# Attention values in three 64-column matmuls, with one operation that scales and evicts

## The chip, the cores and the metric

The kernel runs on one NeuronCore of a Trainium2 chip. The metric is device time in microseconds (us), the median of several executions; smaller is better. Engines are named as in the profile: PE is TensorE (matmuls), PEld its weight loads, DVE is VectorE, ACT is ScalarE, POOL is GpSimd, SP is the queue engine that issues nearly all DMA transfers.

## The reference

One encoder layer on x of 2048 x 1024 float32. What matters here is the attention with a forget gate, 16 heads of 64:

```python
def block(args):                       # one block of 128 queries
    logits = (jnp.einsum('bqhd,bkhd->bhqk', q_i, k).astype(jnp.float32) * scale
              + (F_i[..., :, None] - F[..., None, :]))
    logits = jnp.where(k_pos[None, :] <= q_pos[:, None], logits, -jnp.inf)
    p = jax.nn.softmax(logits, axis=-1).astype(v.dtype)
    return jnp.einsum('bhqk,bkhd->bqhd', p, v)
...
x = x + g_m * fox_mixer(h, ...)
x = x + g_f * (jnp.square(jax.nn.relu(h @ w_mlp_in[i])) @ w_mlp_out[i])
```

## The kernel before, in words

Float32 products are made from operands that are split into a high and a low part, and three of the four partial products are added up in PSUM: high by high, high by low, low by high.

The program has two stretches. The first, to about 1509 us of the span, holds the attention. Heads go in eight pairs g. For each pair a sweep over the 2048 rows (`sweep`, L497 to L499) projects rows to q, k and v; the row operands are split by ACT (L416) and POOL (L417). Beside it runs `attention`: for each block i of 128 queries and each head h of the pair, `att_scores` multiplies q with k (L547, L548, a mask at L550) and DVE adds the forget terms and takes row maxima (L554), `att_exp` makes exponentials on ACT (L565, and the float16 high part `ph` at L572), `att_transpose` makes the low part on DVE (L584) and transposes both parts by DMA into `pT` (L592, issued by SP), and `att_values` multiplies them with the values. The second stretch is the dense MLP; the change touches no line of it.

In `att_values` the tile v holds 128 columns for a head: 64 of the values' high part, then 64 of their low part, all float16. For each block b of 128 keys PE loads the transposed high part of the probabilities and multiplies it with all 128 columns (L610), then loads the low part and multiplies it with the 64 high columns alone (L611). So the high by low product gathers in 64 columns of its own. When both heads of a pair are through, DVE adds the two column groups out of PSUM (`tensor_reduce`, L619), and a second operation multiplies with the reciprocal row sums (L621), on POOL for the pairs 0 to 6 and on DVE for the pair 7. A DMA on SP then writes `ot` to `o_d` (L623). The accumulator `po` has two slots, and `pT` has five buffers (NPT = 5): the sixth transpose must wait until PE has read the first.

The order of instructions on each engine is made by a scheduler in the framework, which models durations and moves instructions by priority and readiness; each engine then executes its list in order. Priorities are set by `pri(n)`, and the values' matmuls have offset 0 (PR_PO), the scores' 100 (PR_S). So an edit of one operation can move others, too.

Of the kernel before, what the change touches and what calls it, by code (L numbers as in the profile page):

```python
# [17 lines left out]
F32 = mybir.dt.float32  # L18
# [4 lines left out]
ALU = mybir.AluOpType  # L23
AX = mybir.AxisListType
# [3 lines left out]
P = 128  # L28
# [4 lines left out]
HD = 64  # L33
# [5 lines left out]
NG = NH // 2  # L39
# [21 lines left out]
def fox_layer(ctx, tc, x, c, norm_mix, norm_mlp, w_ada, b_ada, w_mlp_in, w_mlp_out,  # L61
              fox_w_in, fox_b_f, fox_q_norm, fox_k_norm, fox_w_out, out):
    nc = tc.nc
    x = x[0]
    out = out[0]
# [79 lines left out]
    def pri(n):  # L145
        return tc.high_priority(offset=n)
# [38 lines left out]
    with ExitStack() as st:  # L185
        psS = st.enter_context(tc.tile_pool(name="psS", bufs=2, space=PSUM))
        psT = st.enter_context(tc.tile_pool(name="psT", bufs=1, space=PSUM))
        psO = st.enter_context(tc.tile_pool(name="psO", bufs=1, space=PSUM))
# [405 lines left out]
            return pts  # L594

        po_of, n_po = {}, [0]
        po_all = psO.tile([P, 2, 2, P], F32, tag="O", name="po")

        def att_values(g, i, h, st, pts):
            nb = i + 1  # L600
            if h == 0:
                po_of[g, i] = po_all[:, n_po[0] % 2]
                n_po[0] += 1
            po = po_of[g, i]
            for b in range(nb):
                v = vT[g, b // RB][:, b % RB, h, :]
                pT, bb = pts[b * P // PW], b % (PW // P)
                nw = min(PW // P, nb - b + bb)
                with pri(PR_PO):
                    nc.tensor.matmul(po[:, h, :], lhsT=pT[:, bb, :], rhs=v, start=(b == 0), stop=False)  # L610
                    nc.tensor.matmul(po[:, h, 0:HD], lhsT=pT[:, nw + bb, :], rhs=v[:, 0:HD],  # L611
                                     start=False, stop=(b == nb - 1))
                if b % RB == RB - 1:
                    yield
            if h == 1:
                ot = sb.tile([P, 2, HD], F32, tag="ot", name=f"ot{g}_{i}", bufs=2)
                with pri(PR_OT):
                    nc.vector.reciprocal(st[:, 4:6], st[:, 2:4])
                    nc.vector.tensor_reduce(out=ot, in_=po.rearrange("p h (b d) -> p h d b", b=2), axis=AX.X,  # L619
                                            op=ALU.add)  # L620
                (nc.vector if g == NG - 1 else nc.gpsimd).tensor_tensor(  # L621
                    ot, ot, st[:, 4:6].unsqueeze(2).to_broadcast([P, 2, HD]), op=ALU.mult)
                nc.sync.dma_start(o_d[i][:, g * P:(g + 1) * P], ot.rearrange("p h d -> p (h d)"))  # L623
                del po_of[g, i]

        def attention():
            prev, late = None, []
            per = [C0 + 34.0 * (i + 1) for i in range(NT)]
            tot = 2.0 * sum(per)
            for g in range(NG):  # L630
                for i in range(NT):
                    st_ = sb.tile([P, 6], F32, tag="st", name=f"st{g}_{i}", bufs=6)
                    for h in range(2):
                        L = big(f"L{g}_{i}_{h}")
                        pv = iter(())
                        while len(late) > (LAG_S if i < 8 else LAG_L):
                            for _ in pv:
                                pass
                            pv = att_values(*late.pop(0))
                        nch = i // RB + 1  # L640
                        yield (g, i // RB), per[i] / tot / nch
                        for n, _ in enumerate(att_scores(g, i, h, st_, L)):
                            next(pv, None)
                            if n < nch - 1:
                                yield (g, i // RB), per[i] / tot / nch
                        if prev is not None:
                            late.append((*prev[:4], att_transpose(*prev[:3], *prev[4:])))
                        prev = (g, i, h, st_, L, att_exp(g, i, h, st_, L))
                        for _ in pv:
                            pass  # L650
            late.append((*prev[:4], att_transpose(*prev[:3], *prev[4:])))
            while late:
                for _ in att_values(*late.pop(0)):
                    pass
# [52 lines left out]
        for n, (need, dp) in enumerate(attention()):  # L707
# [3 lines left out]
            while need not in done or p_sw < p_att + (min(LEAD, LEAD0 + LEAD * p_att) if p_att < TAPER else LEAD1):  # L711
                d = next(stream, None)
# [421 lines left out]
    for p in range(NE):  # L1134
        a, b = ops.pop((0, "P1", p))
# [153 lines left out]
    for n, st_ in enumerate(steps):  # L1289
        s, prod, p = st_  # L1290
# [12 lines left out]
        if p == 0:  # L1303
            odd = (n // FP) % 2
            for tb in range(RB):
                pool, tag = (psS, "S") if not odd else ((psQ, "Q"), (psT, "T"))[tb // 2]
# [8 lines left out]
        for tb in range(RB):  # L1315
            for q in range(FP - END, FP) if final and p == FP - 1 else (p,):
                a, b = ops[s, prod, q]
# [34 lines left out]
```

## Time and profile before

| what | value |
|---|---|
| median of 3 runs | 2952.03 us (2948.38 to 2961.26) |
| the profiled execution's own time | 2949.7 us |
| its span, first to last instruction | 2948.0 us |
| busy share of the span: PE, PEld, DVE, ACT, POOL | 90%, 76%, 73%, 56%, 51% |
| granted TensorE clock over the span | 0.963 |

Busy shares are means over two stretches with different limits, so the attention is read by itself in what follows, from 124 us (first value matmul) to 1509 us (last eviction). Matmuls overlap in the array, so the duration of one is longer than the distance from its start to the start of the next; where a cost on PE is meant, the distance between starts is what counts.

### The profile page before, as it was taken

What the parts mean: (1) busy time and instruction counts of PE and PEld (TensorE: products, weight loads), DVE (VectorE), ACT (ScalarE), POOL (GpSimd) and SP (SyncE); (2) the same over time, 40 slices, a digit from 0 to 9 for tenths busy, and PEclk for the clock granted to TensorE, in tenths of its full rate; (3) what the DMA queues carried; (4) which work ended last, traced back from release to release, by engine and by line L of the source; (5) the groups of instructions that cost most, each with busy time, mean ns of one, the idle gap of its engine ahead of it and who ended that gap; (6) DMA issues with size and microseconds to landing.
All of it is one profiled execution on the core that took longest, in us unless ns stands there. A gap on an engine that the chain in (4) does not pass through costs nothing. (4 is left out here: it accounts for less than half of the span.)

```text
span 2948.0 us, 46378 instructions
## 1 busy us (share of the span) xinstructions
PE 2664.8 (90%) x15819; PEld 2231.8 (76%) x15819; DVE 2150.5 (73%) x3695; ACT 1646.8 (56%) x2899; POOL 1509.0 (51%) x1116
## 2 busy tenths in 40 slices
PE   4689888888988899888799999998999999999999
PEld 3677777777777787777678778876888878888887
DVE  6679887898878787887823486667556576875677
ACT  4466666667666676776624256644555444444433
POOL 2354454645445464644533565585654484730464
PEclk9799999998999999999899999999999999999999
DMA  8479999999999999897977867697665684555434
GB/s 283 127 169 191 211 210 210 204 206 209 214 202 216 200 207 200 182 202 161 210 207 234 264 225 236 208 337 238 202 196 175 224 276 126 157 164 169 128 120 155
DMA packets 921070, 593.73 MB, mean 201 GB/s; under 512 B 596276, under 2 KB 776572, under 8 KB 920832
## 3 DMA queue, kind: packets, MB, share of 16 engines
q1 hardware_dynamic: 917248, 578.44, 76.9%
q0 software_dynamic: 3584, 12.32, 1.2%
q8 instruction: 124, 2.03, 0.3%
q14 instruction: 114, 0.93, 0.1%
HBM read 338.81 MB, written 109.19 MB: 152 GB/s over the span
## 5 line engine op out<-in xcount | busy, mean ns | idle before, releaser
L584 DVE SCALAR_TENSOR_TENSOR ph<-L,ph 128x1024 f16<-128x1024 f32 (+7 forms) x384 | 435.0, 1144 | 80.8 <-ACT ph L572 78.9
L417 POOL TENSOR_TENSOR hl<-hl,hh 128x1024 fp32r<-128x1024 f32 x120 | 298.8, 2491 | 250.2 <-ACT hh L416 217.8
L572 ACT ACTIVATE ph<-L 128x1024 f16<-128x1024 f32 (+7 forms) x384 | 302.2, 804 | 172.8 <-DMA pT<-ph 142.8
L497 PE MATMUL psq<-w,hh 128*128 128x384 f32 (+1 forms) x960 | 343.1, 358 | 27.5 <-DVE v L506 12.3
L554 DVE CUSTOM_DVE_ANT_0 L<-S,F 128x1024 f32<-128x1024 f32 (+7 forms) x384 | 343.6, 905 | 22.4 <-PE S L548 8.3
L499 PE MATMUL psq<-w,hl 128*128 128x384 f32 (+1 forms) x960 | 354.6, 371 | 4.5 <-POOL hl L417 4.4
L565 ACT ACTIVATE L<-L,st 128x128 f32<-128x128 f32 (+15 forms) x256 | 306.9, 1199 | 84.9 <-DVE st L559 80.3
L498 PE MATMUL psq<-w,hh 128*128 128x384 f32 (+1 forms) x960 | 342.4, 359 | 6.6 <-POOL w L343 6.6
L142 PE MATMUL yP<-obP,oaP 128*128 128x512 f32 x880 | 343.3, 390 | 3.9 <-DVE obP L757 3.9
L143 PE MATMUL yP<-obP,oaP 128*128 128x512 f32 x880 | 342.5, 389 | 0.0
L141 PE MATMUL yP<-obP,oaP 128*128 128x512 f32 x880 | 338.1, 389 | 2.0 <-ACT obP L756 2.0
L610 PE MATMUL po<-v,pT 128*128 128x128 f16 x2176 | 274.7, 227 | 64.4 <-DMA pT<-ph 56.6
L757 DVE TENSOR_TENSOR oaP<-aP,oaP 128x512 fp32r<-128x512 f32 x220 | 219.6, 998 | 143.9 <-ACT oaP L756 143.7
L547 PE MATMUL S<-kT,qT 128*128 128x512 f32 (+3 forms) x640 | 260.2, 408 | 65.8 <-DVE mx L554 58.4
L756 ACT CAST oaP<-aP 128x512 fp32r<-128x512 f32 x220 | 137.1, 623 | 290.4 <-PE yP L143 275.1
L610 PEld LDWEIGHTS <-pT 128*128 128x128 f16 x2176 | 203.1, 102 | 95.0 <-DMA pT<-ph 67.0
L611 PE MATMUL po<-v,pT 128*128 128x64 f16 x2176 | 257.0, 200 | 0.0
L548 PE MATMUL S<-kT,qT 128*128 128x512 f32 (+3 forms) x640 | 239.6, 382 | 0.0
L611 PEld LDWEIGHTS <-pT 128*128 128x128 f16 x2176 | 196.6, 101 | 41.1 <-issue 30.4
L497 PEld LDWEIGHTS psq<-w,hh 128*128 128x128 f32 x960 | 190.7, 199 | 33.1 <-ACT hh L416 14.4
L141 PE MATMUL mP<-T,wP 128*128 128x512 f32 x512 | 201.4, 394 | 4.7 <-DVE u L1053 2.6
L142 PE MATMUL mP<-T,wP 128*128 128x512 f32 x512 | 200.7, 392 | 0.0
(273 smaller groups left out, 6799.9 us busy)
## 6 DMA issues: line engine op xcount, KB each, us to landing
hl<-hT_d SPq DMA_DIRECT2D x120, 512.0 KB
w_Y_A<-in_w_mlp_in_dram SPq DMA_DIRECT2D x128, 256.0 KB
aP<-s_d SPq DMA_DIRECT2D x128, 256.0 KB
a_d<-c SPq DMA_DIRECT2D x95, 256.0 KB
aP<-a_d SPq DMA_DIRECT2D x92, 256.0 KB
F<-nF_d SPq DMA_DIRECT2D x64, 256.0 KB
wa<-in_w_ada_dram SPq DMA_DIRECT2D x32, 512.0 KB
w_X_A<-in_w_mlp_in_dram SPq DMA_DIRECT2D x64, 256.0 KB
```

The source lines that it names most:

```text
L141: nc.tensor.matmul(ps, lhsT=a[0], rhs=b[0], start=first, stop=False)
L142: nc.tensor.matmul(ps, lhsT=a[0], rhs=b[1], start=False, stop=False)
L143: nc.tensor.matmul(ps, lhsT=a[1], rhs=b[0], start=False, stop=last)
L497: nc.tensor.matmul(ps[:, :n], lhsT=hh, rhs=w[:, 0, :n], start=(kb == 0), stop=False)
L498: nc.tensor.matmul(ps[:, :n], lhsT=hh, rhs=w[:, 1, :n], start=False, stop=False)
L499: nc.tensor.matmul(ps[:, :n], lhsT=hl, rhs=w[:, 0, :n], start=False, stop=(kb == KB - 1))
L554: nc.vector.tensor_tensor_reduce(out=L[:, c0:c1], in0=s2[:, :c1 - c0], in1=Fb[g, h, cch // 2][:, :c1 - c0], scale=1.0, scalar=-3.0e38, op0 ...
L565: nc.scalar.activation(L[:, :W], L[:, :W], AF.Exp, bias=st[:, h:h + 1], scale=1.0, accum_out=st[:, 2 + h:3 + h])
L572: nc.scalar.activation(ph[:, :w], L[:, s0:s0 + w], AF.Copy, scale=PSCALE)
L584: nc.vector.scalar_tensor_tensor(ph[:, w:w + c], L[:, s0:s0 + c], PSCALE, ph[:, :c], op0=ALU.mult, op1=ALU.subtract)
L610: nc.tensor.matmul(po[:, h, :], lhsT=pT[:, bb, :], rhs=v, start=(b == 0), stop=False)
L611: nc.tensor.matmul(po[:, h, 0:HD], lhsT=pT[:, nw + bb, :], rhs=v[:, 0:HD], start=False, stop=(b == nb - 1))
```

## The change

The high part of the probabilities now meets the values' high columns (L610) and their low columns (L611) in two matmuls, each with a weight load of its own, and the low part follows at L612. All three add into the same 64 columns of `po`. The DVE reduction and the multiplication behind it become one DVE operation for every pair, which reads `po`, multiplies by the reciprocal sums and writes `ot`. The DMA that writes `ot` is unchanged (now L621).

```diff
-        po_all = psO.tile([P, 2, 2, P], F32, tag="O", name="po")
+        po_all = psO.tile([P, 2, 2, HD], F32, tag="O", name="po")
...
-                    nc.tensor.matmul(po[:, h, :], lhsT=pT[:, bb, :], rhs=v, start=(b == 0), stop=False)
-                    nc.tensor.matmul(po[:, h, 0:HD], lhsT=pT[:, nw + bb, :], rhs=v[:, 0:HD],
+                    nc.tensor.matmul(po[:, h, :], lhsT=pT[:, bb, :], rhs=v[:, 0:HD], start=(b == 0), stop=False)
+                    nc.tensor.matmul(po[:, h, :], lhsT=pT[:, bb, :], rhs=v[:, HD:2 * HD], start=False, stop=False)
+                    nc.tensor.matmul(po[:, h, :], lhsT=pT[:, nw + bb, :], rhs=v[:, 0:HD],
                                      start=False, stop=(b == nb - 1))
...
                     nc.vector.reciprocal(st[:, 4:6], st[:, 2:4])
-                    nc.vector.tensor_reduce(out=ot, in_=po.rearrange("p h (b d) -> p h d b", b=2), axis=AX.X,
-                                            op=ALU.add)
-                (nc.vector if g == NG - 1 else nc.gpsimd).tensor_tensor(
-                    ot, ot, st[:, 4:6].unsqueeze(2).to_broadcast([P, 2, HD]), op=ALU.mult)
+                    nc.vector.tensor_tensor(ot, po, st[:, 4:6].unsqueeze(2).to_broadcast([P, 2, HD]), op=ALU.mult)
```

The scheduler makes a new order of it. Two places show how. The first is on PE, in the values of pair 4, block 7, head 1 (`pT4_7_1`), where they stand between projections of the next pair (`psq5`, L497 to L499, float32 operands). Before:

```order
L498 MATMUL psq5_0_0_10608<-w5_6_10272,hh5_0_10489 128x384
L499 MATMUL psq5_0_0_10608<-w5_6_10272,hl5_0_10487 128x384
L497 MATMUL psq5_0_0_10608<-w5_7_10277,hh5_0_10489 128x384
L610 LDWEIGHTS pT4_7_1_0_10725
L610 MATMUL po_461<-v4_0_8502,pT4_7_1_0_10725 128x128
L498 MATMUL psq5_0_1_10738<-w5_6_10272,hh5_1_10605 128x384
L611 LDWEIGHTS pT4_7_1_0_10725
L611 MATMUL po_461<-v4_0_8502,pT4_7_1_0_10725 128x64
L498 MATMUL psq5_0_0_10608<-w5_7_10277,hh5_0_10489 128x384
```

And of the change:

```order
L499 MATMUL psq5_0_2_11950<-w5_0_11269,hl5_2_11800 128x384
L497 MATMUL psq5_0_2_11950<-w5_1_11274,hh5_2_11802 128x384
L498 MATMUL psq5_0_2_11950<-w5_1_11274,hh5_2_11802 128x384
L612 LDWEIGHTS pT4_7_1_0_11792
L612 MATMUL po_461<-v4_0_9295,pT4_7_1_0_11792 128x64
L610 LDWEIGHTS pT4_7_1_0_11792
L610 MATMUL po_461<-v4_0_9295,pT4_7_1_0_11792 128x64
L611 LDWEIGHTS pT4_7_1_0_11792
L611 MATMUL po_461<-v4_0_9295,pT4_7_1_0_11792 128x64
L499 MATMUL psq5_0_2_11950<-w5_1_11274,hl5_2_11800 128x384
L497 MATMUL psq5_0_2_11950<-w5_2_11279,hh5_2_11802 128x384
```

Single value matmuls between projections have become groups of three between groups of three, and the same values stand beside later projections (`psq5_0_2` in place of `psq5_0_0` and `psq5_0_1`). Counted over PE's whole list: a matmul on float32 operands stands directly behind one on 16-bit operands 684 times before and 856 times now; from the first to the last value matmul of a head stand 5.5 other matmuls on average before and 7.8 now; and a head's first value matmul stands 12 other matmuls later than before, where the scores moved by less than one.

The second place is POOL, at the same time of the program (`hl5` are rows of the next pair that are split, `ot4` the outputs, `qn4` and `qT4` the normalised queries). Before:

```order
L439 TENSOR_TENSOR qn4_3_10633<-qk4_3_10080,y_q4_3_10586 128x1024
L417 TENSOR_TENSOR hl5_2_10733<-hl5_2_10733,hh5_2_10735 128x1024
L621 TENSOR_TENSOR ot4_7_10916<-ot4_7_10916,st4_7_10530 128x128
L451 CAST qT4_3_10595<-qT4_3_10595 64x512
L417 TENSOR_TENSOR hl5_3_10864<-hl5_3_10864,hh5_3_10866 128x1024
```

And of the change:

```order
L439 TENSOR_TENSOR qn4_3_11686<-qk4_3_11089,y_q4_3_11635 128x1024
L417 TENSOR_TENSOR hl5_2_11800<-hl5_2_11800,hh5_2_11802 128x1024
L451 CAST qT4_3_11644<-qT4_3_11644 64x512
L417 TENSOR_TENSOR hl5_3_11945<-hl5_3_11945,hh5_3_11947 128x1024
```

The multiplication that stood between the splits is gone, and with it the place at which POOL waited for DVE's reduction.

## Rows read from the trace of the kernel before

**Rows 1.** Busy time of each engine in the attention, with granted clock and DMA share

```profile
core 0: us, PE busy (x) PEld busy (x) DVE busy (x) ACT busy (x) POOL busy (x), PEclk, DMA share, GB/s
124.00:1509.00 1385.00, 1198.47 (x9294) 1025.85 (x9295) 1145.43 (x2289) 924.63 (x1541) 716.56 (x542) 0.94 0.96 199
```

**Rows 2.** Who PE waited for in the attention: total us, times, longest

```profile
PE S L547 <- DVE mx L554: 58.1, 50, 4.5
PE po L610 <- DMA pT<-ph: 56.6, 40, 5.8
...
PE po L610 <- DVE ot L619: 7.8, 8, 3.4
...
PE psq L499 <- POOL hl L417: 4.4, 6, 1.7
```

**Rows 3.** What SP's queue waited for in the attention: total us, times, longest

```profile
SPq L592 <- PE po L611: 141.1, 96, 5.5
...
SPq L623 <- POOL ot L621: 24.4, 19, 4.9
```

**Rows 4.** Timeline of PE, values in a row: start, us of one

```profile
905.38 0.23 PE L610 MATMUL po<-v,pT 128*128 128x128 f16 x1 [3.02 <-DMA pT<-ph]
905.44 0.19 PE L611 MATMUL po<-v,pT 128*128 128x64 f16 x1
905.47 0.22 PE L610 MATMUL po<-v,pT 128*128 128x128 f16 x1
...
906.04 0.19 PE L611 MATMUL po<-v,pT 128*128 128x64 f16 x1
906.07 0.42 PE L499 MATMUL psq<-w,hl 128*128 128x384 f32 x1
```

**Rows 5.** Timeline of PE, values between projections: start, us of one

```profile
911.83 0.34 PE L499 MATMUL psq<-w,hl 128*128 128x384 f32 x1
912.01 0.34 PE L497 MATMUL psq<-w,hh 128*128 128x384 f32 x1
912.19 0.23 PE L610 MATMUL po<-v,pT 128*128 128x128 f16 x1
912.23 0.42 PE L498 MATMUL psq<-w,hh 128*128 128x384 f32 x1
912.49 0.20 PE L611 MATMUL po<-v,pT 128*128 128x64 f16 x1
```

**Rows 6.** Timeline of PE's weight loads at the same place

```profile
912.49 0.10 PEld L611 LDWEIGHTS <-pT 128*128 128x128 f16 x1
912.49 0.20 PEld L498 LDWEIGHTS psq<-w,hh 128*128 128x128 f32 x1
912.61 0.19 PEld L499 LDWEIGHTS psq<-w,hl 128*128 128x128 f32 x1
```

**Rows 7.** Groups by line in the attention: count, busy us, mean ns, idle before

```profile
L621 POOL TENSOR_TENSOR ot<-ot,st 128x128 f32<-128x128 f32 x112 | 77.8, 696 | 127.9 <-DVE ot L619 57.0 <-DVE st L559 30.7 <-issue 21.8
...
L619 DVE TENSOR_REDUCE ot<-po 128x128 f32<-128x256 f32 x128 | 53.3, 416 | 21.8 <-PE po L611 17.6 <-issue 3.1 <-DMA o_d<-ot 0.6
...
L506 DVE SCALAR_TENSOR_TENSOR v<-psq,vsc,v 128x128 f16<-128x128 f32 x120 | 41.2, 343 | 24.6 <-ACT v L505 24.2
...
L621 DVE TENSOR_TENSOR ot<-ot,st 128x128 f32<-128x128 f32 x16 | 7.7, 482 | 0.1
```

**Rows 8.** Instructions of L621: ns min/median/max, first and last start

```profile
L621 DVE TENSOR_TENSOR ot<-ot,st x16: 277/293/1985, 1349.1 to 1508.6; 128x128 f32<-128x128 f32 x16
```

## Prediction

> **What bounds the kernel now.** I read the attention by itself, since no line of the MLP behind it changes. First the busy times of its 1385 us: PE 1198 (87%), DVE 1145 (83%), ACT 925, POOL 717, and the DMA engines at a mean share of 0.96 [rows 1]. No single engine is full; three are close to it and wait for each other. PE is the busiest, with 187 us idle (1385 - 1198). Second, the view of waits says what ends PE's idle time: 58.1 us are scores that wait until DVE has cleared a PSUM slot, 56.6 us are values that wait for their transpose [rows 2]. Third, SP's waits: 141.1 us, 96 times, the transposes stand behind the value matmuls, because a `pT` buffer has to come free [rows 3]. So values, transposes and DVE form a ring, and the time of the attention is set by it, with PE closest to the bound. An edit of a few us on one engine reaches the end only in part.
>
> **Third matmul, same columns.** Before, a block costs one step of 128 columns and one of 64; now three of 64, the same 192 columns, with one more weight load. In a row of values, the starts at 905.38, 905.44 and 905.47 say that the step behind a 128-column matmul is 0.06 us and behind a 64-column one 0.03 us, and a weight load stands in each of them; the eight pairs from 905.38 to 906.07 take 0.69 us, 0.086 each [rows 4]. From 0.028 for the 64-column step (the rest of 0.086 once 0.058 is taken off for 128 columns; the starts are read to 0.01), three make 0.084. Over 2176 blocks that is -4 us to 0. I take 0: the extra load is hidden behind the 64 columns of the matmul before it, as it already is at every L611 to L610 step. If that cover failed, each of 2176 loads would show; this is the rival "loads in the open" below.
>
> **More changes between 16-bit and float32.** A projection that follows another starts 0.18 us after it (911.83 to 912.01), but the matmul after a projection that follows a value starts 0.26 us behind that projection (912.23 to 912.49) [rows 5]; at the end of the long row of values the projection at 906.07 stands in the same place [rows 4]. The cause is in the weight loads: the float32 load begins only at 912.49, when the last 16-bit matmul starts, and the next load begins 0.12 us later at 912.61 [rows 6]; the short matmul in front is too short to hide it. So each return from values to float32 costs 0.26 - 0.18 = 0.08 us. The new order has 856 such places instead of 684, 172 more: 172 x 0.08 = 13.8 us more on PE. At most places the new groups of three still stand between projections, so nothing else covers it. How much of it reaches the end? All of it if PE is the bound there, none if PE would have waited anyway. Bounds 0 and +14; I take half, +7, since PE was idle for 187 us in the stretch but for short waits, scattered over hundreds of places.
>
> **Reduction and multiplication become one DVE operation.** Removed on DVE: 128 reductions of 416 ns, 53.3 us, and 16 multiplications, 7.7 us; removed on POOL: 112 multiplications, 77.8 us, and the 127.9 us that POOL stood idle ahead of them, mostly for DVE [rows 7]. Added on DVE: 128 operations on 128 elements with one operand in PSUM and one in SBUF. No row shows exactly that. Nearest are 343 ns for the eviction of v at L506, which also reads 128 elements of PSUM and one SBUF tile, and L621 on DVE, all in SBUF, median 293 and mean 482 ns [rows 7, 8]. I take 343: 43.9 us, so DVE is relieved of 53.3 + 7.7 - 43.9 = 17.1 us; with 293 it is 23.5, with 482 it is -0.7, no relief. POOL's relief is worth little by itself: PE waited for POOL's splits only 4.4 us [rows 2]. DVE's relief can reach PE where scores wait for DVE: in proportion 17.1/1145 of 58.1 us, under 1 us, at most the 17.1 whole. The new operation waits for the last value matmul, as the reduction did; what stands behind it on DVE is the same work. The 7.8 us that PE waited for a `po` slot may halve, since the slot is free after 343 ns instead of 416 and no sooner. I take -4 for all of this, between 0 and -21 (17.1 and half of 7.8).
>
> **The chain to the output.** `o_d` now waits for DVE alone, not for DVE and then POOL. SP stood 24.4 us in 19 places for it, with transposes queued behind [rows 3]. Against that, the values themselves stand 12 matmuls later in PE's list, so `pT` buffers come free later while the transposes that want them stand where they were. I set these two against each other at 0, and make a rival of each.
>
> **Sum.** +7 (half of 13.8) + 0 - 4 + 0 = +3 us on the profiled execution's own 2949.7, 2952.7. That execution lay 2.3 us below the median of the three runs (2952.03), so the median becomes 2955. A measurement of this kernel can tell about 0.5%, 15 us, from no change; the forecast is no change that can be told.
>
> **Rivals.**
> "Ring tightens", slower. The values of a head are spread over 7.8 other matmuls instead of 5.5 and end later, so a buffer of `pT` is held longer by 2.3 x 0.18 = 0.4 us, plus what the shift of 12 matmuls adds, up to 12 x 0.18 = 2.2 us where the ring has no slack. SP's 96 waits for L611 [rows 3] would each grow by 0.4, 38 us in all; if half reaches the end and all 14 us of the changes between types do, 2949.7 + 2.3 + 19 + 14 = 2985 us. It decides when SP's waits behind the value matmuls exceed about 180 us and PE's waits for `pT` rise above 56.6 by as much as 15. For it: DMA at 0.96. Against it: transposes were waited for by PE in only 40 places, so the ring has slack in most.
>
> "Waits go", faster. With POOL out of the chain the 24.4 us of SP go, and PE reaches the values later, so that most of its 56.6 us for `pT` are over when it comes. Say SP's 24.4 are gained, no other wait takes their place, and DVE's relief pays in part: 2952 - 24 + 7 - 5 = 2930. For it: the 12 matmuls of delay are 2.2 us, and a wait is 56.6/40 = 1.4 us long. Against it: the transposes are themselves held by those values.
>
> "Loads in the open", slower. If three 16-bit loads in a row took turns as float32 loads do, 0.12 us apart [rows 6], the third load would cost 0.12 - 0.03 = 0.09 us, 2176 x 0.09 = 196 us on PE. With half of it at the end the time is about 3050 us. Against it stands that a 16-bit load already fits in a 0.03 us step, eight times in that row [rows 4]. The Trainium skill bears on this: "TensorE: Matmul & The Clock Gate", section "Back-to-back issue gap", gives about 81 ns for each pair of weight load and matmul of 128 columns in a sustained stream, whatever the columns alone would take. By that rule the added pair costs 2176 x 81 ns = 176 us on PE, an estimate from that page; the trace disagrees, with 0.06 us for such a step [rows 4].
>
> **How the numbers follow.** No change that can be told: 0.48, 2938 to 2967. "Ring tightens": 0.26, 2967 to 3000. "Waits go": 0.22, 2915 to 2938. "Loads in the open": 0.04. So faster 0.22, same 0.48, slower 0.30. The range leaves out the loads in the open and the far half of the tails of the two rivals, about 0.2 in all: 2925 to 2985.
>
> **What would show it.** In the profile after: value matmuls of 64 columns that start 0.03 us apart in a row (else the loads are in the open); PE's busy time of the attention up by some 10 us or less, at nearly the same span; the eviction near 343 ns, x128, and POOL some 78 us less busy; SP's wait for `ot` gone or on DVE, small; SP's waits behind the value matmuls about 140 us and PE's waits for `pT` about 57. The prediction is wrong if one of these last two moves by more than 15 us and the span of the attention with it, or if the reordering changes the idle time of PE in a way that none of these rows names.

## The result, and the profile after

The change is slower: 2968.03 us median of 8 runs (2962.12 to 2976.36) against 2948.0 us of before, also 8 runs; ratio 1.0067, 95% interval 1.0049 to 1.0084, some 20 us. The profiled execution of the change took 2976.36 us, the longest of the eight, with a span of 2974.7 us, 26.7 more than before.

All of it is in the attention. The last eviction of before starts at 1508.6 us [rows 8], that of the change at 1535.4, 26.8 us later; the MLP behind it takes the same time. The view of L620 in the change (ns min/median/max, first and last start) shows the place and the new operation's price:

```profile
L620 DVE TENSOR_TENSOR ot<-po,st x128: 228/284/293, 137.3 to 1535.4; 128x128 f32<-128x128 f32 x128
```

The busy times of that stretch, the line that answers to [rows 1]:

```profile
core 0: us, PE busy (x) PEld busy (x) DVE busy (x) ACT busy (x) POOL busy (x), PEclk, DMA share, GB/s
124.00:1535.70 1411.70, 1227.89 (x11469) 1029.71 (x11470) 1125.67 (x2273) 925.39 (x1542) 634.79 (x430) 0.94 0.95 196
```

PE is busy 29.4 us longer, DVE 19.8 and POOL 81.8 shorter. PE's idle time is what it was, 183.8 us after 186.5. So the relief of two engines paid nothing that can be seen here, and PE's busy time grew by about what the stretch grew. Busy time also holds the longer step at a return to float32 (a float32 matmul directly behind a 16-bit one) and all that runs at half clock.

The traces take these apart. A step is the distance from the start of one matmul on PE to the next start. If each step is set at the mean of its kind (line, shape, 16-bit or float32 neighbours) over all traces here, at 2.4 GHz and with no wait in it, the sum is PE's steps at full clock. It is 26.5 us longer in the change: 12.2 us in the value matmuls (84.5 ns for a block before, 90.1 now) and 14.3 us in all others, which is about what 172 returns at 0.08 us come to. The time at 1.2 GHz is 165.7 us before and 166.3 now. So in this pair of executions PE's own steps grew by as much as the attention.

What the extra matmul does in a row of values is seen in PE's timeline (start, us of one), where three share a block and each has a weight load of its own:

```profile
929.18 0.19 PE L612 MATMUL po<-v,pT 128*128 128x64 f16 x1
929.21 0.19 PE L610 MATMUL po<-v,pT 128*128 128x64 f16 x1
929.24 0.19 PE L611 MATMUL po<-v,pT 128*128 128x64 f16 x1
929.27 0.19 PE L612 MATMUL po<-v,pT 128*128 128x64 f16 x1
929.30 0.19 PE L610 MATMUL po<-v,pT 128*128 128x64 f16 x1
929.33 0.19 PE L611 MATMUL po<-v,pT 128*128 128x64 f16 x1
929.36 0.42 PE L497 MATMUL psq<-w,hh 128*128 128x384 f32 x1
929.62 0.20 PE L612 MATMUL po<-v,pT 128*128 128x64 f16 x1
```

The steps are 0.03 us each, so a block takes 0.09 us here, close to the 0.086 of before [rows 4]. The last two lines show a return to float32: the projection takes 0.26 us, as in [rows 5].

The waits moved. PE in the change, answering to [rows 2] (total us, times, longest):

```profile
PE S L547 <- DVE mx L554: 82.6, 79, 4.8
PE po L610 <- DMA pT<-ph: 41.1, 27, 6.3
...
PE po L610 <- DVE ot L620: 2.8, 4, 1.3
```

PE waits 15.5 us less for transposes and 24.5 us more for DVE to clear a slot of the scores. DVE is late because of what it waits for. Before, and not yet shown, then in the change, the groups of DVE's low part (L584) and of ACT's float16 high part (L572), with the idle time ahead of each and what ended it:

```profile
L584 DVE SCALAR_TENSOR_TENSOR ph<-L,ph 128x256 f16<-128x256 f32 (+5 forms) x381 | 434.1, 1150 | 80.8 <-ACT ph L572 78.9
...
L572 ACT ACTIVATE ph<-L 128x256 f16<-128x256 f32 (+4 forms) x381 | 301.2, 808 | 172.8 <-DMA pT<-ph 142.8 <-DVE acc L207 15.7 <-POOL L L588 3.9
```

```profile
L584 DVE SCALAR_TENSOR_TENSOR ph<-L,ph 128x256 f16<-128x256 f32 (+5 forms) x381 | 434.4, 1149 | 132.6 <-ACT ph L572 130.7
...
L572 ACT ACTIVATE ph<-L 128x256 f16<-128x256 f32 (+4 forms) x381 | 302.9, 807 | 224.2 <-DMA pT<-ph 193.1 <-DVE acc L207 25.1 <-issue 2.5
```

Read backwards, this could be a chain: ACT waits 50 us more for a transpose to give back a `ph` buffer, DVE waits 52 us more for ACT, and the scores wait for DVE, which works in order. It tells where the waits moved; it does not tell what cost the time, since PE's idle time did not grow. SP's waits, answering to [rows 3], show the start of the chain hardly changed in sum: the wait behind the value matmuls is as long as before, and the wait for `ot`, now for DVE, is not much shorter than the 24.4 us for POOL.

```profile
SPq L592 <- PE po L612: 139.5, 88, 5.2
...
SPq L621 <- DVE ot L620: 20.7, 12, 4.7
```

### The profile page after: what moved, and what is told of

Same layout as the page of the kernel before. It is cut to its first block, busy times and chain, and to the rows that moved or that the text cites. A ratio compares the mean times of both kernels' runs of the same rounds, so it can differ in the third digit from the quotient of the medians.

```text
span 2974.7 us, 50548 instructions
## 1 busy us (share of the span) xinstructions
PE 2697.5 (91%) x17995; PEld 2237.1 (75%) x17995; DVE 2128.1 (72%) x3679; ACT 1647.4 (55%) x2899; POOL 1430.5 (48%) x1004
## 5 line engine op out<-in xcount | busy, mean ns | idle before, releaser
L584 DVE SCALAR_TENSOR_TENSOR ph<-L,ph 128x1024 f16<-128x1024 f32 (+7 forms) x384 | 435.4, 1142 | 132.6 <-ACT ph L572 130.7
L572 ACT ACTIVATE ph<-L 128x1024 f16<-128x1024 f32 (+7 forms) x384 | 303.9, 803 | 224.2 <-DMA pT<-ph 193.1
L497 PE MATMUL psq<-w,hh 128*128 128x384 f32 (+1 forms) x960 | 340.8, 356 | 27.5 <-DVE v L506 12.3
L499 PE MATMUL psq<-w,hl 128*128 128x384 f32 (+1 forms) x960 | 357.4, 375 | 2.0 <-POOL hl L417 2.0
L547 PE MATMUL S<-kT,qT 128*128 128x512 f32 (+3 forms) x640 | 265.6, 416 | 93.6 <-DVE mx L554 83.2
L610 PE MATMUL po<-v,pT 128*128 128x64 f16 x2176 | 276.9, 198 | 45.2 <-DMA pT<-ph 41.1
L754 ACT CAST oaP<-aP 128x512 fp32r<-128x512 f32 x220 | 137.0, 623 | 292.3 <-PE yP L143 280.2
L612 PE MATMUL po<-v,pT 128*128 128x64 f16 x2176 | 278.1, 200 | 0.0
L611 PE MATMUL po<-v,pT 128*128 128x64 f16 x2176 | 276.8, 198 | 0.0
L610 PEld LDWEIGHTS <-pT 128*128 128x128 f16 x2176 | 206.8, 102 | 69.6 <-DMA pT<-ph 48.3
L612 PEld LDWEIGHTS <-pT 128*128 128x128 f16 x2176 | 205.2, 101 | 57.6 <-issue 46.2
L548 PE MATMUL S<-kT,qT 128*128 128x512 f32 (+3 forms) x640 | 242.2, 387 | 0.0
L547 PEld LDWEIGHTS S<-kT,qT 128*128 128x128 f32 x640 | 129.2, 202 | 124.8 <-DVE mx L554 76.6
L611 PEld LDWEIGHTS <-pT 128*128 128x128 f16 x2176 | 207.0, 102 | 15.1 <-issue 11.9
```

The costliest lines, as they stand in the source:

```text
L497: nc.tensor.matmul(ps[:, :n], lhsT=hh, rhs=w[:, 0, :n], start=(kb == 0), stop=False)
L499: nc.tensor.matmul(ps[:, :n], lhsT=hl, rhs=w[:, 0, :n], start=False, stop=(kb == KB - 1))
L547: nc.tensor.matmul(sp, lhsT=q[:, h, qs], rhs=k[:, h, :w], start=True, stop=False)
L584: nc.vector.scalar_tensor_tensor(ph[:, w:w + c], L[:, s0:s0 + c], PSCALE, ph[:, :c], op0=ALU.mult, op1=ALU.subtract)
L610: nc.tensor.matmul(po[:, h, :], lhsT=pT[:, bb, :], rhs=v[:, 0:HD], start=(b == 0), stop=False)
L611: nc.tensor.matmul(po[:, h, :], lhsT=pT[:, bb, :], rhs=v[:, HD:2 * HD], start=False, stop=False)
```

## The experiments

Three theories stood against each other. A: PE pays for its matmuls and for each return from 16-bit to float32 matmuls, and that reaches the end in full. B: the shorter chain to the output upset the waits. C: the third weight load and matmul cost the loss wherever they stand. A fourth, D, came up with the first results: the place of the values in PE's list decides, through the ring of values, transposes and buffers. Most runs shape the order by the priority offset of the value matmuls, PR_PO, which is 0 in both kernels. From here on the counts leave the mask's matmuls (L550) out: within a head's values stand 5.1 other matmuls before and 7.3 in the change. The place of the values is counted in matmuls from the head's first score to its first value, value matmuls left out: 95 before and 107 in the change.

**The matmuls alone.** The eviction goes back to two operations:

```diff
-                    nc.vector.tensor_tensor(ot, po, st[:, 4:6].unsqueeze(2).to_broadcast([P, 2, HD]), op=ALU.mult)
+                    nc.vector.tensor_copy(ot, po)
+                (nc.vector if g == NG - 1 else nc.gpsimd).tensor_tensor(
+                    ot, ot, st[:, 4:6].unsqueeze(2).to_broadcast([P, 2, HD]), op=ALU.mult)
```

> The three 64-column matmuls alone: DVE copies the accumulator out and the multiplication stays on POOL (DVE for the last pair), as before. Returns from 16-bit to float32 matmuls in PE's list: 852 (684 before, 856 in the change). Theory A, PE pays in full: about 0.1 us for each of the 168 returns added, plus 3 to 5 ns for each of 2176 blocks, 24 to 28 us of PE work, and all of it reaches the end: ratio to before 1.006 to 1.010, as slow as the change. Rival B, waits: what costs is that POOL no longer stands between DVE and the output and DVE, ACT and the transposes fall out of step; then this kernel, with the old chain, is within 0.2% of before.

Measured: ratio to before 1.008 (1.0067 to 1.0093). The loss comes with the matmuls and their order.

**The eviction alone.** Before, with one line at L619:

```diff
-                    nc.vector.tensor_reduce(out=ot, in_=po.rearrange("p h (b d) -> p h d b", b=2), axis=AX.X,
-                                            op=ALU.add)
-                (nc.vector if g == NG - 1 else nc.gpsimd).tensor_tensor(
-                    ot, ot, st[:, 4:6].unsqueeze(2).to_broadcast([P, 2, HD]), op=ALU.mult)
+                    nc.vector.tensor_tensor(ot, po[:, :, 0:HD], st[:, 4:6].unsqueeze(2).to_broadcast([P, 2, HD]),
+                                            op=ALU.mult)
```

> The one-operation eviction alone: two matmuls of 128 and 64 columns as before, and the DVE operation reads only the first 64 columns, so the high by low product of the values is left out of the output. Returns in PE's list: 718 (684 before). Theory A: 34 returns at 0.1 us, +3 us, less what DVE's relief of some 17 us pays: ratio 0.998 to 1.002. Rival B: most of the 20 us loss of the change is here, 1.004 to 1.007.

Measured: 0.9994 (0.9982 to 1.0006). B falls: the shorter chain neither costs nor gains anything that can be told. PE waits long for DVE in this run, and it is no slower for it:

```profile
PE S L547 <- DVE mx L554: 88.7, 71, 5.3
PE po L610 <- DMA pT<-ph: 53.4, 35, 6.5
```

**Fewer returns, values early.** Both kernels with one constant changed:

```diff
-PR_S, PR_T, PR_E, PR_PL, PR_PO, PR_OT = 100, 0, 0, 0, 0, 0
+PR_S, PR_T, PR_E, PR_PL, PR_PO, PR_OT = 100, 0, 0, 0, 20, 0
```

> The change with the priority offset of the value matmuls at 20 instead of 0. Returns in PE's list fall from 856 to 488, other matmuls within a head's values from 7.8 to 3.5. Theory A: 368 returns fewer at 0.1 us, 37 us less PE work: ratio to before near 0.994, if the values, now earlier in the list, don't wait longer for their transposes. Rival B: no gain from fewer returns, still 1.005 or more.

> The kernel before with the same offset of 20. Returns fall from 684 to 453. Theory A: 231 fewer at 0.1 us, 23 us: ratio 0.992; and some 10 us faster than the change with the same offset, for 35 returns and the third matmul of 2176 blocks at 3 ns, unless the eviction pays them back. Rival B: within 0.2% of before.

Measured: the change 1.0058 (1.0043 to 1.0073), before 1.0056 (1.0044 to 1.0068). 368 returns fewer gain the change nothing, 231 fewer make before slower, which neither theory had, and the two kernels are equal. A in its plain form falls. Part of the time went the way of the caveat in the expectation: with the first value only 83 matmuls behind the scores in the change, PE meets transposes that have not landed. Its stretch and its waits in the change with offset 20:

```profile
124.00:1524.71 1400.71, 1198.62 (x11454) 1050.47 (x11455) 1133.88 (x2276) 924.79 (x1543) 636.86 (x428) 0.93 0.95 197
...
PE po L610 <- DMA pT<-ph: 92.4, 61, 5.6
...
PE S L547 <- DVE mx L554: 50.7, 42, 3.7
```

PE waits 92.4 us for transposes instead of 41.1, while scores wait less, and its idle time is 202.1 us instead of 183.8. Another part came back in the granted clock (it stands behind the five busy times; 1.00 is 2.4 GHz, and the mean falls with the time at 1.2 GHz): over the whole span and all executions it was 0.957 and 0.953 with offset 20, where before had 0.960 beside them. Against before, the two profiled executions have steps at full clock that are 12 and 22 us shorter, but 39 and 59 us more at 1.2 GHz.

**The order of before, with the third matmul.** The change with PR_PO = 2, and with PR_PO = 6.

> The change with the priority offset of the value matmuls at 2, which gives PE's list nearly the shape of before: 708 returns (684 before, 856 in the change), 5.1 other matmuls within a head's values (5.1 before, 7.3 in the change), first value 97 matmuls behind the head's scores (95 before, 107 in the change). Theory A, returns and the third matmul cost PE time: 24 returns at 0.1 us and 2176 blocks at 3 to 5 ns remain, 9 to 13 us: ratio to before 1.002 to 1.004. Rival C, the third weight load and matmul cost the whole 20 us wherever they stand: 1.006 to 1.008.

> The change with the offset at 6: 534 returns, first value 94 matmuls behind the scores, as before (95). Theory A alone, with PE as the bound: 150 returns fewer than before, 16 us less, and 6 to 11 us more for the third matmul: ratio 0.996 to 0.999. Rival D, the ring of values and transposes gives the saved PE time back as longer waits, as with an offset of 20: 1.002 to 1.006, with PE's idle time in the attention well above 186 us.

Measured: offset 2 gives 0.9982 (0.9967 to 0.9997), offset 6 gives 1.0008 (0.9996 to 1.0021). Both lie outside what any theory had given. C falls: with PE's list shaped as before, three matmuls for each block are as fast as two, if anything a little faster. Offset 6 has 174 returns fewer than offset 2 and gains nothing by them. The stretch with offset 2:

```profile
124.00:1504.63 1380.63, 1200.04 (x11463) 1032.40 (x11464) 1112.78 (x2268) 924.71 (x1540) 648.46 (x430) 0.94 0.96 200
```

PE is busy 1200 us with all 6528 value matmuls, as long as before with 4352 [rows 1]. That does not make the third matmul free on PE: the steps at full clock are 11 us longer than before, nearly all in the values. They were made up by 10 us less in the rest of PE's busy time, with 155.4 us at 1.2 GHz instead of 165.7, and by 6 us less idle time.

**More and less work on PE.** A fourth matmul (the line of L611 twice, PR_PO = 1), and two (that line left out, PR_PO = 0).

```diff
                     nc.tensor.matmul(po[:, h, :], lhsT=pT[:, bb, :], rhs=v[:, HD:2 * HD], start=False, stop=False)
+                    nc.tensor.matmul(po[:, h, :], lhsT=pT[:, bb, :], rhs=v[:, HD:2 * HD], start=False, stop=False)
```

> The change with a fourth 64-column matmul for each block: the high by low product is added twice, so the output counts it twice. Offset 1, which keeps PE's list like that of the change: 859 returns (856), first value 113 behind the scores (107). PE's work rises by 2176 times 0.03 us, 64 us. Theory A, all PE work reaches the end: ratio 1.006 + 0.022 = 1.028. Rival D, half of it is taken up by the 180 us that PE is idle: 1.017.

> The change without the high by low product: two 64-column matmuls for each block, so that product is left out of the output. 737 returns. Against the kernel with the one-operation eviction alone (718 returns, one matmul of 128 and one of 64 columns) it takes 2176 times 64 columns, 0.028 us each, 61 us, off PE and nothing else. Theory A: ratio to before 0.9994 - 0.020 = 0.979 to 0.981. Rival D, PE is not the bound once its work shrinks: 0.99 to 1.0, with idle time of PE up by the difference.

Measured: four 1.0227 (1.0211 to 1.0244), two 0.9919 (0.9905 to 0.9933). Against the change, 64 more columns for each block cost 0.016, about 47 us of the 64 worked out; against the eviction alone, 64 columns fewer gain 0.0075, about 22 us of 61. So PE's columns are paid for, by three quarters when they are added and by a third when they are taken away. Four lies between A and D, two within D. Neither run holds the order exactly: the first value stands at 113 instead of 107 and, counted in the traces, at 92 instead of 97. In the traces the clock takes part of each: the steps at full clock are 62 us longer with four, with 43 us less at 1.2 GHz, and 57 us shorter with two, with 27 us more at 1.2 GHz and 12 us more idle time.

**Returns alone.** Four matmuls with PR_PO = 3 and 4, where the values stand 1 and 4 matmuls further behind the scores than with four and offset 1 (113).

> Four matmuls for each block as in the run with four (the high by low product counted twice), offset 3: 725 returns instead of 859, first value 114 matmuls behind the scores instead of 113, so only the returns differ. Theory A, a return costs 0.1 to 0.13 us of PE time and PE time reaches the end: 134 fewer, 14 to 17 us, ratio to before 1.017 to 1.018 instead of 1.0227. Rival D, the place of the values in the list is what counts: 1.022 to 1.024.

> The same with offset 4: 625 returns instead of 859, first value 117 matmuls behind the scores. Theory A: 234 returns fewer, 24 to 30 us, ratio 1.013 to 1.0145. Rival D: 1.022 or more.

Measured: 1.021 (1.0185 to 1.0236) with 134 returns fewer, 1.0194 (1.0174 to 1.0213) with 234 fewer, against 1.0227. That is 5 and 10 us, about 0.04 us for a return, a third of what A said; the intervals overlap that of the run they are compared with, so the size is uncertain and zero is not excluded. Both lie between A and D. The clock was lower where returns were fewer. The stretch with four and offset 1, then with offset 3:

```profile
124.00:1574.88 1450.88, 1267.54 (x13640) 1082.19 (x13641) 1124.23 (x2263) 925.53 (x1537) 637.95 (x430) 0.96 0.94 190
```

```profile
124.00:1582.07 1458.07, 1272.13 (x13637) 1106.27 (x13635) 1127.80 (x2260) 924.49 (x1536) 645.05 (x430) 0.94 0.93 189
```

With fewer returns the mean clock is 0.94 instead of 0.96, and PE's busy time does not fall, though its steps at full clock are 13 us shorter. Over all executions the clock of the whole span was 0.969 with offset 1, 0.966 with offset 3 and 0.964 with offset 4.

**Place alone.** The change with PR_PO = 2, and the values asked for one head later:

```diff
-AHEAD, LEAD, LAG_S, LAG_L = 1, 0.7, 3, 2
+AHEAD, LEAD, LAG_S, LAG_L = 1, 0.7, 4, 3
```

> The change with offset 2 and the values asked for one head later (LAG_S 4, LAG_L 3 instead of 3, 2): 719 returns, as in the run with offset 2 (708), but the first value stands 107 matmuls behind the scores and the last 113, as in the change (107, 115). Only the place differs from the run with offset 2. If returns are what cost in the change: ratio 0.998 to 1.001. If the later place is, through buffers that come free later: 1.004 to 1.007, with longer waits of ACT and of SP for transposes and their buffers.

Measured: 1.0073 (1.006 to 1.0087), at the upper end of what the later place was expected to cost, against 0.9982 with the values at their old place. Returns are nearly equal (719 and 708), so it is the later place, with the order that comes of it, that costs some 27 us here. The waits with offset 2 alone, then the stretch and the waits of this run:

```profile
ACT ph L572 <- DMA pT<-ph: 162.9, 99, 6.6
DVE ph L584 <- ACT ph L572: 110.5, 96, 6.0
...
PE S L547 <- DVE mx L554: 74.6, 64, 5.5
...
PE po L610 <- DMA pT<-ph: 49.7, 28, 6.3
...
SPq L592 <- PE po L612: 127.0, 77, 5.5
```

```profile
124.00:1533.39 1409.39, 1215.48 (x11463) 1044.84 (x11464) 1110.11 (x2263) 924.47 (x1537) 642.45 (x430) 0.93 0.95 195
...
ACT ph L572 <- DMA pT<-ph: 159.3, 114, 4.2
DVE ph L584 <- ACT ph L572: 100.0, 95, 4.5
...
PE S L547 <- DVE mx L554: 89.9, 71, 4.4
...
PE po L610 <- DMA pT<-ph: 36.1, 27, 3.0
...
SPq L592 <- PE po L612: 150.7, 98, 5.9
```

SP waits 23.7 us longer behind the value matmuls, and PE waits little for transposes and long for DVE, as in the change. The links between did not show: ACT's wait for a `ph` buffer, which the expectation also named, did not grow (162.9 us with offset 2, 159.3 here), and DVE's wait for ACT fell from 110.5 to 100.0. Of the 28.8 us by which this attention is longer than with offset 2, 13.3 are idle time of PE and 15.4 busy time. The steps at full clock are the same to 1 us, but 194.6 us ran at 1.2 GHz instead of 155.4. So a good part of what the later place cost in these two executions is clock; over all executions it was 0.962 here and 0.965 with offset 2.

**Another order with the same counts.** The change with PR_S = 80 instead of 100.

> The change with the scores' priority offset at 80 instead of 100: another order with the same counts (853 returns instead of 856, first value 107 behind the scores in both, 7.0 other matmuls within a head's values instead of 7.3). If these counts decide: 1.005 to 1.008, like the change. If the loss is a chance of one order: anywhere from 0.998 to 1.010, away from the change by more than both intervals.

Measured: 1.0034 (1.0022 to 1.0046). Slower than before, but less than the change by 0.0033, with intervals that do not touch. So the counts do not decide alone; about half of the change's loss hangs on this one order. In the profiled executions of the two, the attention differs by only 4.9 us, with 137.0 us at 1.2 GHz instead of 166.3; another 8.4 us lie in the MLP behind it (1430.6 and 1439.0 us), which no line of either edit touches. This is one execution of each.

Put by the place of the first value behind the scores. The fifth column splits the attention of the profiled execution, in us: PE's steps at full clock, the rest of its busy time (the time lost at 1.2 GHz and short waits inside a step), its idle time. The sixth is the time at 1.2 GHz.

| kernel | place | returns | PE waits for `pT` / `mx`, us | steps / rest / idle | at 1.2 GHz | ratio to before |
|---|---|---|---|---|---|---|
| change, offset 20 | 83 | 488 | 92.4 / 50.7 | 1092 / 107 / 202 | 205 | 1.0058 |
| before, offset 20 | 85 | 453 | 84.7 / 55.1 | 1082 / 116 / 199 | 225 | 1.0056 |
| change, offset 6 | 94 | 534 | 66.7 / 70.8 | 1098 / 89 / 192 | 151 | 1.0008 |
| before | 95 | 684 | 56.6 / 58.1 | 1104 / 95 / 187 | 166 | 1 |
| change, offset 2 | 97 | 708 | 49.7 / 74.6 | 1115 / 85 / 181 | 155 | 0.9982 |
| eviction alone | 97 | 718 | 53.4 / 88.7 | 1105 / 100 / 187 | 182 | 0.9994 |
| change, scores 80 | 107 | 853 | 33.3 / 87.2 | 1130 / 88 / 189 | 137 | 1.0034 |
| change | 107 | 856 | 41.1 / 82.6 | 1130 / 98 / 184 | 166 | 1.0067 |
| change, offset 2, later | 107 | 719 | 36.1 / 89.9 | 1116 / 99 / 194 | 195 | 1.0073 |
| matmuls alone | 109 | 852 | 29.4 / 83.5 | 1129 / 93 / 197 | 156 | 1.008 |

Early values make PE wait for transposes, late values make it wait for DVE. All four kernels near 95 are within 0.2% of before, and all six others are slower, whatever their returns. The two waits alone do not sort the kernels: the eviction alone waits longer for DVE (88.7 us) than the change and loses nothing. Nor do PE's steps: they are shortest where the values are early, and there the clock and the idle time take back more than they save.

## Why the prediction was right or wrong

The time lay in the range, 2968 in 2925 to 2985, but the likeliest case, no change that can be told, did not come: +20 us instead of +3. The time falls at the near end of "Ring tightens", 2967 to 3000, without the signs that this rival named, so that the range held is partly luck. The prediction's own signs went against it: PE's busy time was to rise by some 10 us or less and rose by 29.4; the eviction was to take 343 ns and took 282; and PE's wait for `pT`, which was to stay within 15 us, fell by 15.5 while the attention grew by 26.7.

**The third matmul**, taken at 0: the cover held, the size was off. "Loads in the open" did not come; steps of 0.03 us in the timeline show it. The 81 ns that the Trainium skill's "TensorE: Matmul & The Clock Gate" gives in "Back-to-back issue gap" for a load and a matmul of 128 columns is not seen here; 64 columns with a load took 0.03 us, 128 took 0.06. But counted over all values the steps at full clock are 12 us longer in the change and 11 us with offset 2, outside the bounds of -4 to 0. Whether they reach the end depends on the order: with offset 2 the time is 0.9982.

**The returns**, 172 at 0.08 us, half of it, +7: on PE the 14 us are there in the steps. How much reaches the end is about half by the runs with only returns changed, 172 x 0.04 = 7 us, within their wide intervals.

**The eviction**, -4 between 0 and -21: the run alone gives 0.9994, 2 us, no difference that can be told. The operation took 282 ns in the mean, not 343, so DVE was relieved by more than the 17 us taken (61.0 - 36.1 = 24.9), and that still bought nothing that can be told.

**"I set these two against each other at 0"**: this step failed. The chain to the output was worth nothing (eviction alone; SP still waits 20.7 us for `ot`), but the new order was worth some 25 us: the same edit takes 1.0067 with the scheduler's order and 0.9982 with offset 2. In the profiled executions of these two, 2976 and 2946 us, the steps at full clock make up 15 us of the difference, most of it by the returns, the rest of PE's busy time 13 and its idle time 3. That the later place can cost such a time without more returns is shown in a run that moves the values as far as the change did, 27 us, though by another means, asking for them a head later. How the loss of the change divides between place, returns and clock is not shown.

**The rival's own test** was not met. It wanted SP's waits behind the values above 180 us and PE's waits for `pT` up; they stood at 139.5 and 41.1. That PE's wait for `pT` fell fits later values, whose transposes had more time to land. The chain through the other end of the ring, buffers that come free late hold ACT, ACT holds DVE, DVE holds the scores, can be read in the waits of the change, but the runs do not bear it out as the cause: in the run with place alone neither ACT's nor DVE's wait grew, and in the change PE was idle no longer than before.

Open: what in the later place lowers the clock or costs time, and why an order with the same counts lost only half as much. The three counts used here don't tell these orders apart, and it wasn't tried further.

## What to carry to other kernels

When a scheduler makes the order, an edit has two effects, its own and that of the new order, and each can be timed by itself: here the edit in an order like that of before cost nothing that can be told, in the order of the scheduler 0.7%, and one priority offset was the difference. In this ring the values had a best place behind the scores: earlier, PE waited for transposes itself; later, it waited for DVE and the time rose, but the waits alone did not say by how much. Two orders are compared by PE's steps, its clock and its idle time apart, since one can give back what another saves. Before a saving on a busy engine is counted, look at what it waits for: relief of 25 us on DVE and 80 us on POOL gave nothing that can be told here.

## What the runs showed of the hardware that had not been expected

Float16 weight loads of 128 x 128 are hidden behind 64 columns for as long as the row lasts: in a row the median step is 29 ns behind 64 columns and 57 ns behind 128, so two matmuls of 64 columns cost about what one of 128 does. A return from 16-bit to float32 operands lengthens the next step from 0.18 to 0.26 us, yet taking 134 of them away moved the time by 0.04 us each.

Part of what PE's list saved came back in the granted clock. Over all executions of a kernel it was 0.957 and 0.953 with offset 20 where before had 0.960, 0.957 with two matmuls where before had 0.961, and 0.966 and 0.964 with fewer returns where four matmuls with offset 1 had 0.969. Offset 6, with steps 6 us shorter than before, shows none of it (0.962 and 0.961). The clock also differed where the steps were the same, 0.962 and 0.965 with place alone. Why it differs was not tested.
